# SBUF layout of a split-float matmul kernel: constants at the far end, packs and slots padded to 128 bytes

## The chip, the core and the metric

One core of a Trainium2 chip runs the whole program. The metric is the device time of one execution in microseconds (us), the median of the runs shown. TensorE (PE) multiplies, ScalarE (ACT) and VectorE (DVE) copy, split and combine, GpSimd (POOL) does small sums, SyncE (SP) issues every DMA. Each matmul has a stationary operand (128 columns, loaded first) and a moving operand (128, 256, 258 or 512 columns that stream past it), both read from SBUF.

## What is computed

A two-layer hybrid block (short convolution, gated MLP, sparse attention, convolution branch, then an FFN), followed by one block of another model (mLSTM with a Fourier branch, then a 16-expert MoE), on 256 tokens of width 1024, all in float32:

```python
def hybrid_layer(x, ...):                       # twice
    h = rmsnorm(x, g_mix)
    z = h @ w_in                                # 1024 x 2884
    ...                                         # four mixers y_a .. y_d
    x = x + concatenate([y_a, y_b, y_c, y_d], -1) @ w_out
    hf = rmsnorm(x, g_ffn)
    return x + (silu(hf @ w_gate) * (hf @ w_up)) @ w_down    # hidden 2816
# then rmsnorm, and second_block once:
    y, yc = token_mix(h, hc, lp, with_ctx)      # w_in 1024 x 1536, mLSTM, Fourier, w_out
    x = x + gate1 * rmsnorm_2(y, g_post_mix)
    for e in range(16):                         # hier_moe
        a = silu(h @ w_gate[e]) * (h @ w_up[e])
        y = y + combine[..., e, None] * (a @ w_down[e])
```

## The kernel before

**Split matmuls.** A large product is not done in the slow float32 mode. Each operand is split into a high part (rounded to float32r by ACT, L190) and a low part (the remainder, DVE, L191), and `mm3` (L234 to L241) adds three float32r products: high x high, high x low, low x high, pass by pass over the chunks of the contraction. The names end in `h`/`hi` and `l`/`lo`: `whi`, `wlo` are the weights, `xnh`, `xnl` a layer's input, `hfh`, `hfl` the FFN's input, `ffh`, `ffl` the FFN's hidden activations, `yah` to `ydl` the mixers' outputs, `hh`, `hl` the input of the second block, `m2h`, `m2l` its mixer output, `xgh`, `xgl` the tokens gathered for experts, `ahh`, `ahl` the experts' hidden activations, `oh` the one-hot columns that gather tokens from `h2h`, `h2l`. A plain float32 matmul stands on the timeline as two records.

**Which operand moves.** In `proj` (projections, FFN gate and up) and in the down and out products, the weights are stationary and 256 columns of activations move. In `proj_tok` (v and g_v) and in the whole MoE (L1308, L1335) it is the other way round: activations are stationary, and 256 or 512 columns of `whi`/`wlo` move.

**Stages.** Layer 0, FFN 0, layer 1, FFN 1 (with the ada modulation on DVE and the context's part woven in), the second block's mixer (`mixer2`), the MoE. An FFN has 11 groups: gate and up (96 matmuls of 256 columns), then down of the group before (48). An expert has 24 matmuls of 512 columns each for gate, up and down; the gates and ups are in two weight tiles each, the down too. Each weight tile is a DMA of 1 MB into a `raw` slot, a cast, a subtraction, and then its matmuls.

**Memory and order.** A tile framework places pools on a stack from the left end of SBUF (some, `side="right"`, from the right end) and writes all waits itself; the order on each engine comes from its scheduler with the priorities in the code (`later`). `const`, the first pool, holds small tiles (`ones`, `mhalf`, `inv256`, `warm`, `g0`, the pack `cst0`, `mod`): 3040 bytes of each partition, at the left end. `wraw`, `s8` (the 8 KB slots of the activations), `wsp` (`whi` and `wlo`, three buffers each) and the pools of the stages stack on it. `load_pack` (L174) loads a table of constants or parameters as one tile of as many columns as the table has. `rstd_row` keeps a 2-column tile `rsk` for a layer. The input of the second block has 258 columns a chunk (two more for a shift), so its slot in `s8` is 8256 bytes. `slot` (in `route`) is 8 floats a partition.

Of the kernel before, what the change touches and what calls it, by code (L numbers as in the profile page):

```python
# [11 lines left out]
F32 = mybir.dt.float32  # L12
# [5 lines left out]
P = 128  # L18
# [122 lines left out]
class Build:  # L141
    def __init__(self, ctx, tc, ins, out, offs, dbg=None):
        self.tc, self.nc, self.ins, self.out, self.dbg = tc, tc.nc, ins, out, dbg or {}
        self.offs, self.at = offs, {}
        pool = lambda name, bufs, **k: ctx.enter_context(tc.tile_pool(name=name, bufs=bufs, **k))
        self.const = pool("const", 1)
        self.wraw = pool("wraw", 3)
        self.psum = pool("psum", 1, space=bass.MemoryType.PSUM)
        self.pool = pool
        self.pending = None  # L150
        self.wx, self.wy, self.nraw = None, None, 0
# [20 lines left out]
        nc.scalar.activation(warm, self.ones[:, 0:1], AF.Square)  # L172

    def load_pack(self, name, pool, tag=None, bufs=1):  # L174
        t = pool.tile([P, self.ins[name].shape[1]], F32, tag=tag or name, name=name, bufs=bufs)
        self.nc.sync.dma_start(t, self.ins[name])
        for n, (o, m) in self.offs[name].items():
            self.at[n] = t[:, o:o + m]

    def p(self, name, i=None, n=1):  # L180
        return self.at[name] if i is None else self.at[name][:, i:i + n]
# [110 lines left out]
    def rstd_row(self, ps, n, eps, keep=None, direct=False):  # L292
        nc = self.nc
        if self.pending:
            self.pending()
            self.pending = None
        ms = self.tmp.tile([P, 2], F32, tag="ms", name="ms")
        nc.vector.tensor_scalar(ms, ps[:, 256:258], 1.0 / n, eps, op0=OP.mult, op1=OP.add)
        rs = (keep or self.tmp).tile([P, 2], F32, tag="rsk" if keep else "rs", name="rs", bufs=1 if keep else 2)
        nc.gpsimd.tensor_tensor(rs, ms, self.mhalf[:, 0, 0:2], op=OP.pow)  # L300
        for j in range(2):
            nc.tensor.matmul(ps[:, j * P:(j + 1) * P], rs[:, j:j + 1].to_broadcast([P, P]), self.c("ident"),
                             start=True, stop=True)
        if direct:
            return ps[:, 0:256]
        rb = keep.tile([P, 256], F32, tag="rbk", name="rbk", bufs=1) if keep else \
            self.tmp.tile([P, 256], F32, tag="t1", name="rb", bufs=self.t1)
        nc.scalar.copy(rb, ps[:, 0:256])
        return (rb, rs) if keep else rb
# [15 lines left out]
    def layer(self, l, x, X, sq):  # L325
# [274 lines left out]
        sqm = self.bank()  # L600
        H = self.bighl("hf")
        order = ((0, Ya), (2, Yc), (1, Yb), (3, Yd))
        for n, (j, Y) in enumerate(order):
            W = self.weights(w_out[:, j], 2, 1024, -4)
            for m in SPREAD:
# [4 lines left out]
                if n == 3:  # L610
                    tt(xm[:, m, :], acc[m // 2][:, m % 2, :], x[:, m, :], op=OP.add)
                    self.scaled_split(xm, p(f"g_ffn{l}", m), H, m)
                    self.sum_sq(sqm, xm[:, m, :], m, m == 7, 2)
        self.dump(f"xm{l}", xm)
        return xm, H, sqm

    def ffn(self, l, xm, H, sqm):
        nc, p = self.nc, self.p
# [4 lines left out]
        def gate_up(g):  # L623
            w_g = self.ins["w_gate"][l].rearrange("(k p) c -> p k c", p=P)[:, :, g * 256:(g + 1) * 256]
            w_u = self.ins["w_up"][l].rearrange("(k p) c -> p k c", p=P)[:, :, g * 256:(g + 1) * 256]
            psg = self.proj(self.weights(w_g, 8, 256), H, spread=SPREAD if g == 0 else None)
            if not rbs:
# [5 lines left out]
            nc.vector.tensor_tensor(gt, gt, rbb, op=OP.mult)  # L633
            psu = self.proj(self.weights(w_u, 8, 256), H)
            nc.vector.tensor_tensor(gt, psu, gt, op=OP.mult)
# [257 lines left out]
    def mixer2(self, x, sq):  # L893
# [4 lines left out]
        rb = self.rstd_row(sq, 1024, 1e-6, direct=True)  # L898
        xr = self.big("xr")
        sq2 = self.bank()  # L900
        H = self.bighl("h", (8, 258))
        nc.scalar.copy(H[0][:, :, 256:258], mod[:, 0:8, 0:1].to_broadcast([P, 8, 2]))
        tt(H[1][:, :, 256:258], mod[:, 0:8, 0:1].to_broadcast([P, 8, 2]), H[0][:, :, 256:258].bitcast(F32), op=OP.subtract)
        W = [self.weights(self.w_in2[:, :, g * 256:(g + 1) * 256], 8, 256, -4) for g in range(2)]
# [303 lines left out]
    def route(self):  # L1208
        nc, tmp, keep = self.nc, self.tmp, self.act
        small = lambda name, *shape: tmp.tile([P, *shape], F32, tag=name, name=name, bufs=1)  # L1210
        tt = nc.vector.tensor_tensor
        lt = small("lt", 5, 2, 4)
        for j in range(2):
            nc.vector.scalar_tensor_tensor(lt[:, :, j, :], self.lg[:, j * 20:(j + 1) * 20].rearrange("p (b i) -> p b i", b=5),
                                           self.rs2[j], self.brow.rearrange("p (b i) -> p b i", b=5),
                                           op0=OP.mult, op1=OP.add)
        v = lt.rearrange("p b j i -> p (b j) i")
        rank = self.ranks(v[:, 0:2], 2, "g")
        asg = tmp.tile([P, 2, 4], FR, tag="asg", name="asg", bufs=1)
        nc.vector.tensor_scalar(asg, rank, 0.0, None, op0=OP.is_equal)  # L1220
        own = asg.bitcast(F32)
        ps = self.bank()
        nc.tensor.matmul(ps[:, 0:8], self.striu, asg.rearrange("p j g -> p (j g)"), start=True, stop=False,
                         skip_group_check=True)
        nc.tensor.matmul(ps[:, 4:8], self.onesr, asg[:, 0], start=False, stop=True, skip_group_check=True)
        self.slot = keep.tile([P, 2, 4], F32, tag="slot", name="slot")
        nc.vector.tensor_scalar(self.slot, own, -1000.0, 1000.0, op0=OP.mult, op1=OP.add)
        self.slotted = tt(self.slot, self.slot, ps[:, 0:8].rearrange("p (j g) -> p j g", j=2), op=OP.add)
        for j in range(2):
            nc.tensor.matmul(ps[:, 8:12], self.onesr, asg[:, j], start=j == 0, stop=j == 1, skip_group_check=True)  # L1230
        gm, pe, psel = small("gm", 2), small("pe", 2, 4), small("psel", 2)
        nc.vector.tensor_reduce(gm, v[:, 0:2, :], AX.X, OP.max)
        tt(pe, v[:, 0:2, :], gm[:, :, None].to_broadcast([P, 2, 4]), op=OP.subtract)
        nc.scalar.activation(pe, pe, AF.Exp)
        nc.vector.tensor_reduce(psel, pe, AX.X, OP.add)
        nc.vector.reciprocal(psel, psel)
        ve = v[:, 2:]
        rank = self.ranks(ve, 8, "e")
        top, second = small("top", 8, 4), small("second", 8, 4)
        c1, c2, w1, w2 = small("c1", 8, 4), small("c2", 8, 4), small("w1", 8), small("w2", 8)  # L1240
        nc.vector.tensor_scalar(top, rank, 0.0, None, op0=OP.is_equal)
        nc.vector.tensor_scalar(second, rank, 1.0, None, op0=OP.is_equal)
        for w, c, o in ((w1, c1, top), (w2, c2, second)):
            tt(c, ve, o, op=OP.mult)
            nc.vector.tensor_reduce(w, c, AX.X, OP.add)
        tt(w2, w2, w1, op=OP.subtract)
        nc.scalar.activation(w2, w2, AF.Exp)
        nc.vector.tensor_scalar(w1, w2, 1.0, None, op0=OP.add)
        nc.vector.reciprocal(w1, w1)
        tt(w1.rearrange("p (g j) -> p g j", j=2), w1.rearrange("p (g j) -> p g j", j=2),  # L1250
           psel[:, None, :].to_broadcast([P, 4, 2]), op=OP.mult)
        tt(w2, w2, w1, op=OP.mult)
        for w, c, o in ((w1, c1, top), (w2, c2, second)):
            tt(c, o, w[:, :, None].to_broadcast([P, 8, 4]), op=OP.mult)
        tt(c1, c1, c2, op=OP.add)
        comb = small("comb", 2, 4, 4)
        tt(comb, c1.rearrange("p (g j) i -> p j g i", j=2), own[:, :, :, None].to_broadcast([P, 2, 4, 4]), op=OP.mult)
        self.split(comb, *(self.idc[:, :, o:o + 16].rearrange("p j (g i) -> p j g i", g=4) for o in (P, P + 16)))
        self.over = keep.tile([P, 5], mybir.dt.int32, tag="over", name="over")
        mxc = small("mxc", 1)  # L1260
        nc.vector.tensor_reduce(mxc, ps[:, 8:12], AX.X, OP.max)
        nc.vector.tensor_scalar(self.over[:, 0:4], ps[:, 8:12], 128.0, None, op0=OP.is_gt)
        nc.vector.tensor_scalar(self.over[:, 4:5], mxc, 128.0, None, op0=OP.is_gt)
# [287 lines left out]
```

## Time and profile before

| | us |
|---|---|
| three runs | 1147.66, 1145.09, 1141.58 |
| median | 1145.09 |
| span of the profiled execution, first to last instruction (its only time on the page) | 1141.0 |
| PE busy in it | 1081.2 (95%) |
| DVE busy | 894.8 (78%) |
| ACT busy | 644.1 (56%) |
| DMA engines, share of the span | 63.7% |

The profiled execution is 0.4% below the median and inside the three runs' own spread. A matmul's duration on the page is from its start to the end of its result, and neighbours overlap; what a stream of matmuls costs is the distance from start to start, which is read from the timeline: the start of the row after, less the start of the row, divided by the count.

### The profile page before, as it was taken

What the parts mean: (1) busy time and instruction counts of PE and PEld (TensorE: products, weight loads), DVE (VectorE), ACT (ScalarE), POOL (GpSimd) and SP (SyncE); (2) the same over time, 40 slices, a digit from 0 to 9 for tenths busy, and PEclk for the clock granted to TensorE, in tenths of its full rate; (3) what the DMA queues carried; (4) which work ended last, traced back from release to release, by engine and by line L of the source; (5) the groups of instructions that cost most, each with busy time, mean ns of one, the idle gap of its engine ahead of it and who ended that gap; (6) DMA issues with size and microseconds to landing.
All of it is one profiled execution on the core that took longest, in us unless ns stands there. A gap on an engine that the chain in (4) does not pass through costs nothing.

```text
span 1141.0 us, 18470 instructions
## 1 busy us (share of the span) xinstructions
PE 1081.2 (95%) x7384; PEld 981.0 (86%) x7384; DVE 894.8 (78%) x1449; ACT 644.1 (56%) x937; POOL 131.7 (12%) x139
## 2 busy tenths in 40 slices
PE   7998999999999989999999989899899999999995
PEld 6897999999998979899999988877778888878783
DVE  6897677887777976866877778765599898998976
ACT  5635654343455364635563345743587778777763
POOL 3091010000020830410000022000100000000001
PEclk9998999999999999999999989899989999999998
DMA  8734448677755254656678860420679699999981
GB/s 268 244 111 153 144 149 274 239 252 250 258 179 164 85 174 151 201 202 212 232 239 280 290 208 22 145 74 1 240 281 362 236 322 341 344 344 372 315 308 41
DMA packets 142126, 248.34 MB, mean 218 GB/s; under 512 B 6608, under 2 KB 84816, under 8 KB 142032
## 3 DMA queue, kind: packets, MB, share of 16 engines
q1 hardware_dynamic: 142032, 247.08, 63.7%
q8 instruction: 60, 0.98, 0.3%
q14 instruction: 34, 0.28, 0.1%
HBM read 246.01 MB, written 1.05 MB: 217 GB/s over the span
## 4 chain that ended last, share of the span: by engine, by line
PE 46%; DVE 4%; ACT 2%; issue 1%; POOL 1%; POOLq 0%; ACTq 0%; DVEq 0%
PE mm L240 24%; PE acc L240 14%; DVE wlo L191 1%; PE acc L919 1%; PE mm L1351 1%; PE mm L1278 1%; PE mm L729 1%; PE mm L1325 1%; PE mm L801 0%; POOL ssq L278 0%; PE mm L1060 0%; PE mm L1061 0%; PE mm L781 0%; DVE Mt L753 0%; PE mm L784 0%
## 5 line engine op out<-in xcount | busy, mean ns | idle before, releaser
L190 ACT CAST whi<-raw 128x1024 fp32r<-128x1024 f32 (+2 forms) x375 | 406.6, 1126 | 271.5 <-PE mm L240 130.8
L191 DVE TENSOR_TENSOR wlo<-raw,whi 128x1024 fp32r<-128x1024 f32 (+2 forms) x375 | 483.5, 1323 | 79.9 <-ACT whi L190 79.4
L240 PE MATMUL mm<-hfh,whi 128*128 128x256 f32 x672 | 94.6, 282 | 0.0
L240 PE MATMUL mm<-hfh,wlo 128*128 128x256 f32 x672 | 93.8, 282 | 0.0
L240 PE MATMUL mm<-hfl,whi 128*128 128x256 f32 x672 | 91.5, 278 | 0.0
L278 POOL TENSOR_TENSOR ssq<-ssq,sqt 128x256 f32<-128x256 f32 x40 | 37.6, 942 | 433.0 <-ACT sqt L270 428.7
L240 PEld LDWEIGHTS mm<-hfh,whi 128*128 128x128 f32 x672 | 85.7, 188 | 0.4 <-ACT whi L190 0.4
L240 PEld LDWEIGHTS mm<-hfh,wlo 128*128 128x128 f32 x672 | 85.4, 188 | 0.0
L240 PEld LDWEIGHTS mm<-hfl,whi 128*128 128x128 f32 x672 | 84.5, 188 | 0.0
L240 PE MATMUL mm<-whi,xgh 128*128 128x512 f32 x256 | 71.7, 399 | 0.5 <-ACT xgh L190 0.4
L240 PE MATMUL mm<-wlo,xgh 128*128 128x512 f32 x256 | 70.3, 395 | 0.0
L240 PE MATMUL acc<-ffh,whi 128*128 128x256 f32 x352 | 70.2, 280 | 0.0
L240 PE MATMUL mm<-whi,xgl 128*128 128x512 f32 x256 | 70.1, 395 | 0.0
L240 PE MATMUL acc<-ffh,wlo 128*128 128x256 f32 x352 | 69.8, 280 | 0.0
L240 PE MATMUL acc<-ffl,whi 128*128 128x256 f32 x352 | 69.4, 279 | 0.0
L692 DVE CUSTOM_DVE_ANT_0 araw<-araw,arow 128x1024 f32<-128x1024 f32 x48 | 58.3, 1228 | 0.0
L240 PEld LDWEIGHTS mm<-wlo,xgh 128*128 128x128 f32 x256 | 47.9, 187 | 11.9 <-DVE wlo L191 0.3
L240 PEld LDWEIGHTS mm<-whi,xgl 128*128 128x128 f32 x256 | 48.0, 187 | 11.7
L240 PEld LDWEIGHTS mm<-whi,xgh 128*128 128x128 f32 x256 | 46.9, 188 | 11.8 <-ACT xgh L190 1.3
L240 PEld LDWEIGHTS acc<-ffh,whi 128*128 128x128 f32 x352 | 54.0, 190 | 0.2
L240 PEld LDWEIGHTS acc<-ffh,wlo 128*128 128x128 f32 x352 | 54.1, 191 | 0.0
L240 PEld LDWEIGHTS acc<-ffl,whi 128*128 128x128 f32 x352 | 53.7, 190 | 0.0
(490 smaller groups left out, 2043.9 us busy)
## 6 DMA issues: line engine op xcount, KB each, us to landing
raw<-in_w_gate_dram SPq DMA_DIRECT2D x54, 1024.0 KB, 6.6
raw<-in_w_up_dram SPq DMA_DIRECT2D x54, 1024.0 KB, 6.8
raw<-in_w_down_dram SPq DMA_DIRECT2D x54, 1024.0 KB, 6.5
raw<-in_w_in_dram SPq DMA_DIRECT2D x29, 1024.0 KB, 5.2
araw<-in_w_adaT_dram SPq DMA_DIRECT2D x48, 512.0 KB, 5.0
raw<-in_w_out_dram SPq DMA_DIRECT2D x12, 1024.0 KB, 4.9
x<-in_xT_dram SPq DMA_DIRECT2D x4, 256.0 KB, 3.8
raw<-in_w_in_dram SPq DMA_DIRECT2D x4, 256.0 KB, 4.2
```

Source lines behind the costliest of these rows:

```text
L190: nc.scalar.copy(hi, src)
L191: nc.vector.tensor_tensor(lo, src, hi.bitcast(F32), op=OP.subtract)
L240: self.nc.tensor.matmul(out, w, x, start=start and i == 0, stop=stop and i == n - 1, **kw)
L278: nc.gpsimd.tensor_tensor(self.ssq, self.ssq, sq, op=OP.add)
L692: nc.vector.tensor_tensor_reduce(out, raw, rows[n], 1.0, 0.0, OP.mult, OP.add, self.mod[:, t, n:n + 1])
L729: nc.tensor.matmul(ps[0:100, :], self.weff[:, (c + 4) % 8, :], src, start=c == 0, stop=c == 7)
L919: nc.tensor.matmul(psx[m][:, 0:258], a, b[:, k, :], start=k == 0 and i == 0, stop=k == 7 and i == 2)
L1278: nc.tensor.matmul(ps[:, k * 256:(k + 1) * 256], self.H2[s][:, j, f], oh[:, j].rearrange("p n s -> p (n s)"), start=i == 0, stop=i == 3)
L1325: nc.tensor.transpose(ps[:, m * P:(m + 1) * P], ga[:, m * P:(m + 1) * P], self.c("ident"))
L1351: nc.tensor.matmul(ps, oT[:, j, :], Y[:, s, hf, :], start=s == 0, stop=s == 1)
```

## The change

Constants go to the right end of SBUF; the tables, `rsk` and `slot` get a size that is a multiple of 128 bytes, and so do the slots of `s8`, by way of the 264-column tile:

```diff
-        self.const = pool("const", 1)
+        self.const = pool("const", 1, side="right")
...
-        t = pool.tile([P, self.ins[name].shape[1]], F32, tag=tag or name, name=name, bufs=bufs)
-        self.nc.sync.dma_start(t, self.ins[name])
+        n = self.ins[name].shape[1]
+        t = pool.tile([P, -(-n // 32) * 32], F32, tag=tag or name, name=name, bufs=bufs)
+        self.nc.sync.dma_start(t[:, 0:n], self.ins[name])
...
-        rs = (keep or self.tmp).tile([P, 2], F32, tag="rsk" if keep else "rs", name="rs", bufs=1 if keep else 2)
+        rs = (keep or self.tmp).tile([P, 32 if keep else 2], F32, tag="rsk" if keep else "rs", name="rs",
+                                     bufs=1 if keep else 2)[:, 0:2]
...
-        H = self.bighl("h", (8, 258))
+        H = [t[:, :, 0:258] for t in self.bighl("h", (8, 264))]
...
-        self.slot = keep.tile([P, 2, 4], F32, tag="slot", name="slot")
+        self.slot = keep.tile([P, 2, 4, 4], F32, tag="slot", name="slot")[:, :, :, 0]
```

The instructions and their order are the same on all five engines, row by row. Four waits differ: the load of the pack `par2` loses one on DVE, the cast of `striu` (L1365) loses its waits, the matmul L1223 that uses it gains one on PE, and one 1 MB load of an early `w_up` tile of the MoE gains waits on PE and ACT.

What differs everywhere is where operands start. The built programs place them as follows (bytes, start address modulo 128; every chunk of a tile is a multiple of 128 bytes long unless noted):

| operand | part | before | after |
|---|---|---|---|
| `hfh`, `xnl` | moving, 256 columns | 96 | 0 |
| `hfl`, `xnh` | moving, 256 columns | 32 | 0 |
| `ffh`, `ffl`, `yah` to `ydl` | moving, 256 columns | 32 | 0 |
| `whi`, `wlo` | stationary (layers, FFN) and moving (MoE, `proj_tok`) | 96 | 0 |
| `hh`, `hl` (258 columns, k-th chunk) | moving | 32 + 8k, 96 + 8k | 32k |
| `xnh`, `xnl` in `proj_tok` | stationary | 32, 96 | 0 |
| `xgh`, `xgl` | stationary | 32 | 32 |
| `ahh`, `ahl` | stationary | 96 | 96 |
| `yo`, `oh` | moving | 96, 32 | 96, 32 |

## Rows read from the trace of the kernel before

**Rows 1.** Page, part 1: engine, busy us (share), instructions.

```profile
PE 1081.2 (95%) x7384; PEld 981.0 (86%) x7384; DVE 894.8 (78%) x1449; ACT 644.1 (56%) x937; POOL 131.7 (12%) x139
```

**Rows 2.** Page, part 4: the chain that ended last, by engine.

```profile
PE 46%; DVE 4%; ACT 2%; issue 1%; POOL 1%; POOLq 0%; ACTq 0%; DVEq 0%
```

**Rows 3.** Windows: stretch, length, busy PE, PEld, DVE, ACT, POOL; clock, DMA share, GB/s.

```profile
60.00:115.00 55.00, 49.77 (x397) 44.73 (x396) 44.61 (x98) 26.71 (x51) 26.61 (x29) 0.94 0.43 143
...
618.65:635.43 16.78, 16.78 (x147) 16.78 (x146) 13.11 (x16) 6.89 (x6) 0.00 (x0) 1.00 0.83 281
...
830.00:833.00 3.00, 3.00 (x14) 2.88 (x15) 3.00 (x14) 2.22 (x6) 0.00 (x0) 0.50 1.05 403
...
860.00:928.00 68.00, 68.00 (x305) 54.83 (x305) 62.83 (x65) 52.98 (x61) 0.00 (x0) 1.00 0.86 304
...
996.00:1064.00 68.00, 68.00 (x302) 54.75 (x301) 60.73 (x63) 49.13 (x56) 0.00 (x0) 1.00 0.99 354
```

**Rows 4.** Chain in order of time (start, us, what): FFN 1, mixer, an expert.

```profile
618.65 11.31 PE mm L240 x96
629.96 5.47 PE acc L240 x48
...
705.64 1.67 PE acc L919 x14
...
854.18 5.59 PE mm L240 x24
859.76 5.58 PE acc L240 x24
```

**Rows 5.** PE's timeline in FFN 1: start, us, line, tiles, count.

```profile
598.09 0.39 PE L240 MATMUL acc<-ffh,wlo 128*128 128x256 f32 x2
...
600.81 0.39 PE L240 MATMUL acc<-ffh,wlo 128*128 128x256 f32 x2
...
605.51 1.08 PE L240 MATMUL mm<-hfl,whi 128*128 128x256 f32 x8
606.43 1.12 PE L240 MATMUL mm<-hfh,wlo 128*128 128x256 f32 x8
607.38 1.11 PE L240 MATMUL mm<-hfh,whi 128*128 128x256 f32 x8
```

**Rows 6.** PE's timeline in layer 0: a projection, then plain float32 matmuls.

```profile
60.60 1.07 PE L240 MATMUL mm<-xnh,whi 128*128 128x256 f32 x8
61.51 1.12 PE L240 MATMUL mm<-xnl,whi 128*128 128x256 f32 x8
62.46 1.10 PE L240 MATMUL mm<-xnh,wlo 128*128 128x256 f32 x8
63.40 1.02 PE L375 MATMUL mm<-ropea,cst 128*128 128x512 f32 x2
64.26 1.02 PE L376 MATMUL mm<-ropeb,cst 128*128 128x512 f32 x2
```

**Rows 7.** PE's timeline in w_out: layer 1, first and last of its stretch.

```profile
440.60 0.40 PE L240 MATMUL acc<-ych,whi 128*128 128x256 f32 x2
...
441.78 0.40 PE L240 MATMUL acc<-ych,wlo 128*128 128x256 f32 x2
```

**Rows 8.** The same in layer 0.

```profile
129.04 0.39 PE L240 MATMUL acc<-ych,whi 128*128 128x256 f32 x2
...
131.76 0.39 PE L240 MATMUL acc<-ybh,whi 128*128 128x256 f32 x2
```

**Rows 9.** PE's timeline at the start of the MoE.

```profile
832.33 0.63 PE L1278 MATMUL mm<-oh,h2h 128*128 128x256 f32 x2
832.75 0.84 PE L1278 MATMUL mm<-oh,h2l 128*128 128x256 f32 x3
833.39 0.50 PE L1278 MATMUL mm<-oh,h2h 128*128 128x256 f32 x2
```

**Rows 10.** Who waited for whom on the DMA queue, 780 to 1141 us.

```profile
SPq L227 <- DVE wlo L191: 252.3, 87, 14.5
```

## Prediction

> **What bounds the kernel now.** First the busy shares: PE is busy 1081.2 of 1141.0 us, DVE 894.8, ACT 644.1 [rows 1]. Then the chain that ended last: 46% of the span is PE, 4% DVE, 2% ACT [rows 2]; the parts add up to a little over half, so it is followed back to about the middle of the program, and from there, in the second FFN and in the experts, it is matmul after matmul [rows 4]. The stretches say the same by stage: one FFN group of 16.78 us has PE busy for all 16.78, DVE for 13.11; 68 us of the MoE, four experts, have PE busy for all 68, DVE for 60.73 to 62.83, DMA engines for 0.86 to 0.99 of the time. Only the layers leave PE idle, 49.77 of 55 us [rows 3]. So in FFN and MoE a nanosecond less between two matmuls is a nanosecond less of span, until DVE or DMA is late.
>
> Next, what a matmul costs there. Column counts alone would give the same pace everywhere for 256 columns; the timeline doesn't. In the FFN's down product 24 matmuls (12 rows of two) take 2.72 us from 598.09 to 600.81, 113.3 ns each. In gate and up, eight with `hfh` moving take 0.95 us, 118.75 each, and eight with `hfl` 0.92, 115 each [rows 5]. In a layer `xnh` starts at 113.75, `xnl` runs at 118.75, and the pass after it, `xnh` again, at 117.5 [rows 6]. Held against the placements: a moving operand that starts at 32 of 128 bytes reaches 113.3, one at 96 never does, and after such a pass the one at 32 is slow for a while. At 2.4 GHz 256 columns are 106.7 ns, so 6.6 or 12 ns are lost each time. They are not lost at the low clock: in the stretch with a granted clock of 0.50, which is 1.2 GHz, five 256-column matmuls take 1.06 us, 212 each, and 256 columns at 1.2 GHz are 213 [rows 3, 9]. Nor in plain float32, which takes two cycles a column: 0.86 us for two records of 512 columns are 430 each, 0.42 ns a cycle [rows 6]. What is lost has to do with how fast operands are read at full speed, and there the start address may matter. That is the change's case, and it rests on two offsets, neither of which is 0.
>
> **The change, part by part.** No instruction is added, removed or moved, so every term is a change of pace.
>
> *What one matmul costs at offset 0* the trace does not show. The bounds: not below 107.5 ns for 256 columns and 215 for 512 (float32's 0.42 ns a cycle); above, 118.75 for 256, the pace of `hfh`. I take 113.3, the best that a steady run of split matmuls shows, and the nearest in kind. No 512-column split matmul moves from offset 32; the experts' move from 96 and take 5.59/24 = 232.9 ns in gate and up and 5.58/24 = 232.5 in down [rows 4]. I take two 256-column prices, 226.7.
>
> *FFN.* A group is 11.31 us for 96 gate and up matmuls (117.8 each) and 5.47 for 48 down (114.0 each) [rows 4]. At 113.3 it saves 96 x 4.5 ns + 48 x 0.7 ns = 0.46 us. Two layers of 11 groups: 22 x 0.46 = 10.1 us, all on the path. DVE's 13.11 us a group stay under the 16.3 that are left.
>
> *Layers.* Half a projection is 24 matmuls in 2.80 us [rows 6], 2.72 at 113.3, so a projection saves 0.16 us, the ten in a layer 1.6. `v` and `g_v` move weights, at 96: 96 x 5.4 ns = 0.5 us. w_out has 192 matmuls a layer, at 32 both times; in layer 1 ten take 1.18 us (118 each) and could save 0.9, in layer 0 24 take 2.72 and save nothing [rows 7, 8]. Sum for both layers 3.2 + 1.0 + 0.9 = 5.1 us. PE is idle for a tenth there and waits elsewhere for DVE's chain, so I count 0.7 of it: 3.6.
>
> *Second mixer and context.* 288 matmuls of 258 columns at 119.3 (14 in 1.67 us [rows 4]) against 114.2: 1.5 us, half of it on the path, 0.7. The context's projection, 96 x 5.4 ns = 0.5. w_out_2, 96 of 512 columns at 6 ns, 0.6. Together 1.8.
>
> *MoE.* 768 gate and up matmuls x 6.2 ns and 384 down x 5.8 ns: 4.8 + 2.2 = 7.0 us. What is late next: DVE at 15.2 to 15.7 us an expert (60.73/4, 62.83/4) against PE's 17.0, which would become 16.5; DMA delivers 354 GB/s there with its engines 0.99 busy [rows 3], while 6.29 MB in 16.5 us are 381. But the queue's issues wait for a slot to come free (252 us in all [rows 10]), so transfers follow PE's pace, and I let this gain stand whole.
>
> *The rest at nothing.* The four changed waits: the early `w_up` load that now waits for PE and ACT is queued before loads of the experts; behind it on SP stand only loads whose issues wait for slots anyway [rows 10], so a few us there are hidden, bound 0 to 3 us. ACT and DVE read and write the same tiles at the new offsets too; their durations I leave, since nothing shows an offset in them.
>
> Sum: 10.1 + 3.6 + 1.8 + 7.0 = 22.5 us of 1141.0, that is 1118.5; taken from the median, 4.1 us above that execution, 1145.1 - 22.5 = 1122.6. I say 1122.
>
> **The rivals.** *Full pace.* If a start at 0 takes the whole loss away, 107.5 and 215 ns: FFN 22 x (16.78 - 144 x 0.1075) = 28.6; layers 0.7 x (20 projections x 0.44 + 192 token matmuls x 11.2 ns + w_out 1.1 and 2.0) = 9.8; mixer, context and w_out_2 1.6 + 1.1 + 1.7; the MoE would save 18 ns x 1152 = 20.7 but DVE's 15.7 an expert and the DMA stop it near 16.0 of 17.0, so 16. Sum 59, time 1086. For it: the loss is in reading operands, and both offsets of before are 32 off a multiple of 64. Against it: no row of split matmuls below 113.3. The Trainium skill (TensorE: Matmul & The Clock Gate, Back-to-back issue gap) gives N/2.4 + 2.5 ns, by which 256 columns take 109.2 and 512 take 215.8 and the sum is, as an estimate, 51 us and the time 1094; no split matmul here runs so.
>
> *No change: the pace is a state, not an offset.* w_out in layer 1 runs at 118 for its whole stretch with operands that start at the same 32 and 96 as in layer 0, where it runs at 113.3 [rows 7, 8]. So an offset doesn't settle the pace; moving and stationary reads may fall into one rhythm or another by what ran before. If the new layout gets both, gains and losses cancel: 1145. The skill speaks for this one: by SBUF — State Buffer, Specifications (TRN2), a line of SBUF is 16 bytes, and 32, 96 and 0 are all multiples of 16, so the start of a 256-column operand would cost the same; the rows above, 113.3 against 118.75, don't agree with that as the whole story.
>
> *Slower: equal offsets collide.* Before, the fast case has moving at 32 and stationary at 96, half of 128 apart; `hfh` and `xnl` have both at 96 and run at 118.75. After, in every projection and FFN product both start at 0. If what costs is that both start at the same offset, all of FFN goes to 118.75: 144 x 118.75 = 17.10 us a group, 0.32 more, 22 x 0.32 = +7.0; the layers add 0.7 x (20 projections x 0.10 + w_out 1.05 and 0.14) = +2.2; experts' down, with both at 96, and gate and up, with 96 and 32, run alike today, so +0 there. Time 1154. It decides from 116.5 ns on, the mean of an FFN group today (16.78/144). Against it: the pass of `xnh` over `wlo` at 117.5 and w_out of layer 1 at 118 are slow with unequal offsets [rows 6, 7], so equality is at most one cause.
>
> **How the numbers follow.** Forecast 0.40, full pace 0.18, no change 0.18, equal offsets 0.24. 0.5% of the time, 5.7 us, is about what a measurement here can tell from nothing, so faster 0.58, same 0.18, slower 0.24. From 1090 to 1156 the range leaves out about half of the full pace's cases and a third of the slower ones, 0.17. The forecast alone would be 1112 to 1132.
>
> **What would show it.** Right: the FFN's chain pieces shrink from 11.31 to about 10.9 us for 96 and stay at 5.44 for 48; eight matmuls with `hfh` take 0.91 us on the timeline; 24 of an expert take 5.44. Full pace: 10.4, 5.2 and 5.2, and DVE's weight subtraction or DMA begins to end PE's waits in the MoE. No change: a mixture of 113 and 118 that doesn't follow the operands' names. Equal offsets: 48 down matmuls take 5.7 us. I'd be wrong altogether if the 512-column pace moves the other way from the 256-column one, or if ACT's casts or DVE's subtractions change their durations.

## The result and the profile after

The changed kernel takes a median of 1149.46 us (20 runs, 1145.72 to 1155.25), the kernel before on the same chip 1144.18 us (20 runs). The ratio is 1.0054, 95% interval 1.0038 to 1.0070: slower by some 5 us, where 22 us less were forecast. The profiled execution of the changed kernel took 1153.82 us with a span of 1152.0, 11.0 us longer than the span before.

The page of the changed kernel, busy times and the chain by engine (the counterparts of [rows 1] and [rows 2]):

```profile
PE 1096.2 (95%) x7384; PEld 995.6 (86%) x7384; DVE 895.6 (78%) x1449; ACT 643.4 (56%) x937; POOL 131.5 (11%) x139
...
PE 71%; DVE 11%; issue 6%; POOL 6%; ACT 4%; DMA 1%; SPq 0%; POOLq 0%; DVEq 0%; ACTq 0%
```

DVE, ACT and POOL have the same work as before to within 1 us. PE is busy 15.0 us longer with the same 7384 instructions, so each takes longer. (The chain's shares can't be compared: this one is followed back to the start of the program, the one before only to its middle.)

The chain of the changed kernel in order of time (start, us, what), where [rows 4] have 11.31 and 5.47 in FFN 1, and 5.59 and 5.58 in an expert (L241 is L240 of before):

```profile
627.96 11.52 PE mm L241 x96
639.48 5.76 PE acc L241 x48
...
864.89 5.60 PE mm L241 x24
870.49 5.60 PE acc L241 x24
```

Both FFN pieces are at exactly 120.0 ns a matmul (11.52/96, 5.76/48). A group takes 17.28 instead of 16.78 us, and 22 times 0.50 are 11.0 us. The experts' matmuls of 512 columns have the pace of before, 233 ns.

Where that lands by stage: windows of both kernels, cut where the first matmul of FFN 0, layer 1, FFN 1, the second mixer and the experts begins (columns as in [rows 3]). Before:

```profile
0.00:141.26 141.26, 124.86 (x913) 113.51 (x913) 105.86 (x218) 75.91 (x138) 43.13 (x53) 0.95 0.56 183
141.26:332.50 191.24, 188.92 (x1620) 188.51 (x1618) 151.13 (x176) 83.42 (x81) 7.99 (x8) 1.00 0.72 238
332.50:456.15 123.65, 117.86 (x913) 108.28 (x912) 98.25 (x207) 63.83 (x117) 42.22 (x41) 0.99 0.43 137
456.15:686.61 230.46, 220.55 (x1807) 217.36 (x1805) 169.99 (x233) 117.45 (x148) 22.53 (x19) 0.97 0.68 231
686.61:835.49 148.88, 137.06 (x838) 119.00 (x837) 103.75 (x335) 81.05 (x187) 11.47 (x15) 0.93 0.31 110
835.49:1141.00 305.51, 291.91 (x1306) 234.29 (x1304) 265.81 (x286) 222.46 (x270) 4.32 (x4) 0.98 0.85 296
```

After:

```profile
0.00:142.89 142.89, 127.49 (x913) 115.94 (x914) 105.70 (x218) 75.73 (x138) 42.99 (x53) 0.95 0.55 181
142.89:339.31 196.42, 194.36 (x1619) 193.95 (x1618) 151.30 (x176) 83.23 (x81) 8.01 (x8) 1.00 0.70 232
339.31:463.46 124.15, 119.53 (x914) 110.10 (x912) 98.41 (x207) 63.76 (x117) 42.30 (x41) 0.99 0.42 137
463.46:697.15 233.69, 225.32 (x1806) 222.19 (x1805) 170.64 (x233) 117.24 (x148) 22.36 (x19) 0.97 0.67 227
697.15:846.32 149.17, 137.35 (x838) 119.38 (x837) 103.89 (x335) 81.13 (x187) 11.49 (x15) 0.93 0.31 110
846.32:1152.00 305.68, 292.21 (x1306) 234.05 (x1304) 265.66 (x286) 222.33 (x270) 4.33 (x4) 0.98 0.84 296
```

Layer 0 loses 1.6 us, FFN 0 5.2, layer 1 0.5, FFN 1 3.2, the mixer 0.3, the experts 0.2. In FFN 1 PE is busy 4.8 us longer but waits 1.5 us less, which leaves 3.2.

**Why 11 in the profile and 5 in the medians.** These two executions had the same mean clock, 0.973. Over all executions a straight line through time and granted clock falls by 8.1 us per 0.01 of clock for the changed kernel (20 runs) and 8.4 for the kernel before (67 runs, those beside the experiments up to e9_all64_moe), and at 0.973 the lines stand at 1153.9 and 1143.9 us, 10.0 apart. But the median clock of the changed kernel is 0.978, that of those 67 runs of the kernel before 0.973. Those 0.005 are worth 4 us on the lines. So at one clock the changed kernel is some 10 us slower, and the medians are closer, the executions of the changed kernel having been granted a higher clock. That the slower pace is what raises the clock is a guess: no execution at 0.981 was profiled.

### The profile page after: what moved, and what is told of

It reads as the page before. It is cut to its first block, busy times and chain, and to the rows that moved or that the text cites. A ratio compares the mean times of both kernels' runs of the same rounds, so it can differ in the third digit from the quotient of the medians.

```text
span 1152.0 us, 18470 instructions
## 1 busy us (share of the span) xinstructions
PE 1096.2 (95%) x7384; PEld 995.6 (86%) x7384; DVE 895.6 (78%) x1449; ACT 643.4 (56%) x937; POOL 131.5 (11%) x139
## 4 chain that ended last, share of the span: by engine, by line
PE 71%; DVE 11%; issue 6%; POOL 6%; ACT 4%; DMA 1%; SPq 0%; POOLq 0%; DVEq 0%; ACTq 0%
PE mm L241 37%; PE acc L241 23%; DVE wlo L192 3%; POOL ssq L279 2%; POOL cv L428 1%; POOL ctap L427 1%; ACT whi L191 1%; DVE cv L430 1%; PE acc L417 1%; POOL rs L302 1%; PE acc L921 1%; PE mm L1353 1%; PE mm L1280 1%; PE mm L731 1%; PE mm L304 1%
## 5 line engine op out<-in xcount | busy, mean ns | idle before, releaser
L241 PE MATMUL mm<-hfh,whi 128*128 128x256 f32 x672 | 95.5, 284 | 0.0
L241 PE MATMUL mm<-hfl,whi 128*128 128x256 f32 x672 | 94.6, 283 | 0.0
L241 PE MATMUL mm<-hfh,wlo 128*128 128x256 f32 x672 | 94.3, 283 | 0.0
L241 PEld LDWEIGHTS mm<-hfh,whi 128*128 128x128 f32 x672 | 86.9, 192 | 0.4 <-ACT whi L191 0.4
L241 PEld LDWEIGHTS mm<-hfl,whi 128*128 128x128 f32 x672 | 86.7, 192 | 0.0
L241 PEld LDWEIGHTS mm<-hfh,wlo 128*128 128x128 f32 x672 | 86.7, 192 | 0.0
L241 PE MATMUL acc<-ffh,whi 128*128 128x256 f32 x352 | 72.2, 286 | 0.0
L241 PE MATMUL mm<-whi,xgh 128*128 128x512 f32 x256 | 71.7, 399 | 0.4 <-ACT xgh L191 0.3
L241 PE MATMUL acc<-ffh,wlo 128*128 128x256 f32 x352 | 71.8, 285 | 0.0
L241 PE MATMUL acc<-ffl,whi 128*128 128x256 f32 x352 | 71.5, 285 | 0.0
L241 PE MATMUL mm<-wlo,xgh 128*128 128x512 f32 x256 | 70.4, 396 | 0.0
L241 PE MATMUL mm<-whi,xgl 128*128 128x512 f32 x256 | 70.0, 395 | 0.0
L241 PEld LDWEIGHTS mm<-wlo,xgh 128*128 128x128 f32 x256 | 48.0, 188 | 11.8 <-DVE wlo L192 0.3
L241 PEld LDWEIGHTS mm<-whi,xgl 128*128 128x128 f32 x256 | 48.1, 188 | 11.7
L241 PEld LDWEIGHTS mm<-whi,xgh 128*128 128x128 f32 x256 | 46.9, 188 | 11.9 <-ACT xgh L191 1.3
L241 PEld LDWEIGHTS acc<-ffh,whi 128*128 128x128 f32 x352 | 55.5, 194 | 0.2
L241 PEld LDWEIGHTS acc<-ffh,wlo 128*128 128x128 f32 x352 | 55.6, 194 | 0.0
L241 PEld LDWEIGHTS acc<-ffl,whi 128*128 128x128 f32 x352 | 55.4, 194 | 0.0
```

Of the source, the lines that this page charges most:

```text
L241: self.nc.tensor.matmul(out, w, x, start=start and i == 0, stop=stop and i == n - 1, **kw)
```

## Experiments

The distance of two operands is here the moving operand's start address less the stationary one's. Theory going in: this distance, modulo 128 bytes, sets the pace; the change made it 0 in the projections and the FFN. Rivals: the absolute offset of one of them; no offset at all but a state of the queue; another part of the change.

**m1_map: the pace by offsets, by itself.** Its core (x and w are split once, `mo` and `so` are start offsets in bytes):

```diff
+    x = [t[:, mo // 4:mo // 4 + 2048].rearrange("p (k t) -> p k t", k=kc) for t in X]
+    w = [t[:, so // 4:so // 4 + 2048].rearrange("p (k t) -> p k t", k=8) for t in W]
...
+            for a, b in ((0, 0), (0, 1), (1, 0)):
+                for k in range(kc):
+                    nc.tensor.matmul(o, w[a][:, k, m * P:(m + 1) * P], x[b][:, k, 0:n], ...)
```

> A program of its own that leaves the whole reference out (it writes zeros and one unread product): after one split of a 1024 x 256 input and of a 1024 x 256 weight it runs steady streams of 256-column split matmuls in the three-pass order of L241, 96 at a time, for all 16 pairs of start offsets 0, 32, 64, 96 (mod 128 bytes) of moving and stationary operand, twice in opposite orders, then finer offsets, 512 columns and 128 columns. RELATION theory (only the distance of the two start offsets counts): pairs at equal offsets 120.0 ns a matmul (11.52 us per 96), pairs 64 apart 113.3 (10.88 us per 96), pairs 32 or 96 apart between or at 117.7; the absolute offsets make no difference. ABSOLUTE-MOVING rival: moving at 0 gives 120 and at 32 gives 113.3 whatever the stationary offset. ABSOLUTE-STATIONARY rival: the stationary offset decides alone. STATE rival (offsets don't matter, a queue settles in one of several paces): one pace for all 16 pairs, or paces that follow the order of the streams and differ between the two orders. 512 columns: 232 to 234 ns at all offsets by the rows of before and after.

Its chain in order of time; m is the moving, s the stationary start offset (a, c: 256 columns; d: 512):

```profile
59.36 11.52 PE am0s0z L50 x96
...
82.23 11.31 PE am0s64z L50 x96
...
138.98 11.31 PE am32s96z L50 x96
...
172.79 11.51 PE am64s64z L50 x96
...
452.02 5.44 PE cm112s0z L50 x48
...
463.15 5.45 PE cm192s0z L50 x48
...
497.25 5.68 PE cm16s16z L50 x48
...
530.82 5.45 PE dm32s32z L50 x24
...
541.86 5.60 PE dm32s96z L50 x24
547.46 5.51 PE dm64s0z L50 x24
```

Equal offsets run at 120 at 0, 32, 64 and 96 alike, so neither absolute offset alone decides. One equal pair does not: (16, 16) ran at 118.3, right after a stream at 113.3, and why is open. And 64 apart gives 117.8, not 113.3, with the very pair (32, 96) that the FFN of the kernel before ran at 113.3. 113.3 appears at (112, 0) and (192, 0). And one pair, (32, 0), ran at 117.8, 120.0 and 116.7 in three places; (96, 0), not equal, gave 120. So distance is right about most of the equal pairs, wrong as the whole story. A surprise: 512 columns run fastest at equal offsets, 227.0 against 233 at most others; 64 ahead, at (64, 0), comes near with 229.6.

**e1_w64: weights 64 bytes away.**

```diff
+        ph.enter_context(self.tc.tile_pool(name="gapa", bufs=1)).tile([P, 16], F32, name="gapa")
         self.wsp = ph.enter_context(self.tc.tile_pool(name="wsp", bufs=3))
+        ph.enter_context(self.tc.tile_pool(name="gapb", bufs=1)).tile([P, 16], F32, name="gapb")
...
-        H = [t[:, :, 0:258] for t in self.bighl("h", (8, 264))]
+        H = [t[:, :, 0:258] for t in self.bighl("h", (8, 260))]
```

> The changed kernel with only the weight tiles (whi, wlo) moved by 64 bytes: moving operands stay at 0, stationary at 64 (mod 128); everything behind them is put back by another 64 bytes, and to make room the rows of h are 260 columns long instead of 264. RELATION theory: all the 256-column split matmuls at 113.3 instead of 120.0 ns: an FFN group 16.32 instead of 17.28 us, 22 of them -21 us, layers and mixer some -5 us: 1120 to 1128 us, ratio to the kernel before 0.980 to 0.986. ABSOLUTE-MOVING rival (moving at 0 is the slow one): as the changed kernel, 1149 us, ratio 1.005, pieces of 96 at 11.52 us. STATE rival: somewhere at 117.9, about 1143 us, ratio 1.00.

Measured 1147.11 us, ratio 1.0038 (1.0014 to 1.0062). PE's timeline in FFN 1: first down row of a group, first gate row of the next, next down row:

```profile
599.23 0.40 PE L241 MATMUL acc<-ffh,whi 128*128 128x256 f32 x2
...
604.88 1.08 PE L241 MATMUL mm<-hfh,whi 128*128 128x256 f32 x8
...
616.16 0.40 PE L241 MATMUL acc<-ffh,whi 128*128 128x256 f32 x2
```

48 down matmuls in 5.65 us, 96 gate and up in 11.28: 117.7 and 117.5 ns, better than 120, far from 113.3. My expectation of 113.3 fell; the rival of a state had named 117.9.

**e2_const: only the constants moved.**

```diff
-        self.const = pool("const", 1)
+        self.const = pool("const", 1, side="right")
```

> The kernel before with only the constants moved to the right end: every start offset goes up by 32 mod 128 (weights 96 to 0, hfh and xnl 96 to 0, ff, xnh and hfl 32 to 64), the distances stay. RELATION theory: nothing changes, 1144 us, ratio 1.000 (0.997 to 1.003), pieces of 96 at 11.31 and of 48 at 5.47 us. ABSOLUTE-MOVING rival (0 slow, 32 fast): the pieces of 48 down (moving now at 64, not seen before) anywhere from 5.4 to 5.76 us, those of 96 (two of three passes at 0, the third at 64) at 11.5 us: 1149 us or more.

Measured 1143.77 us, ratio 0.9995 (0.9979 to 1.0011), with every absolute offset of the split matmuls changed and every distance kept. The same three places:

```profile
596.00 0.40 PE L240 MATMUL acc<-ffh,whi 128*128 128x256 f32 x2
...
601.47 1.12 PE L240 MATMUL mm<-hfh,whi 128*128 128x256 f32 x8
...
612.78 0.40 PE L240 MATMUL acc<-ffh,whi 128*128 128x256 f32 x2
```

5.47 and 11.31, the pieces of before. The moving operands `hfh` lie at a multiple of 128 here, and nothing is gained or lost by it.

**e3_eq64: all at 64, equal.**

```diff
+        ph.enter_context(self.tc.tile_pool(name="gapa", bufs=1)).tile([P, 16], F32, name="gapa")
         self.s8 = ph.enter_context(self.tc.tile_pool(name="s8", bufs=4))
...
-        H = [t[:, :, 0:258] for t in self.bighl("h", (8, 264))]
+        H = [t[:, :, 0:258] for t in self.bighl("h", (8, 260))]
```

> The changed kernel with everything from the slots of x on shifted by 64 bytes (rows of h 260 columns long, to make room): moving and stationary operands at 64, so none lies at a multiple of 128, all still at equal offsets. RELATION theory: as the changed kernel, 120.0 ns, pieces of 96 at 11.52 us, about 1149 us, ratio 1.005. ABSOLUTE-MOVING or ABSOLUTE-STATIONARY rival (the multiple of 128 itself is the slow place): 113 to 118 ns, 1120 to 1143 us.

Measured 1152.83 us, ratio 1.0069 (1.0046 to 1.0092); four runs; pieces of 11.47 and 5.76. The down matmuls, all at equal offsets away from 0, cost what they cost at 0. In gate and up only `hfh` is equal to the weights: modulo 256 `hfl` lies 128 away here, and these 96 matmuls take 11.47 instead of 11.52.

**m2_states: what ran ahead.** Streams as in m1_map, each behind a short stream:

```diff
+    for mo in range(0, 256, 16):
+        stream("preEz", 0, 0, 256, 1)
+        stream(f"Em{mo}s0z", mo, 0, 256, 2)
+    for mo in range(0, 256, 16):
+        stream("preFz", 64, 0, 256, 1)
+        stream(f"Fm{mo}s0z", mo, 0, 256, 2)
...
+        stream("Hz", 96, 96, 256, 4, lo=32)
+        stream("Iz", 32, 96, 256, 2)
...
+        stream("Jz", 32, 96, 256, 4)
+        stream("Kz", 32, 96, 256, 2)
```

> A program of its own that leaves the whole reference out, as m1_map. The map showed 120.0 ns at equal offsets, but at others 113.3, 116.7, 117.8, 118.3 or 120.0, and for one pair different paces at different times. Here each moving offset in steps of 16 bytes from 0 to 240 (stationary at 0) follows three predecessors: E, 24 matmuls at equal offsets; F, 24 matmuls 64 bytes apart; G, a wait for VectorE. Then the FFN patterns: H and I have the offsets of the kernel before (hi 96, lo 32, stationary 96; then 48 at 32), J and K have all moving operands 64 from the weights. SEVERAL-PACES theory (offsets allow some paces, the stream ahead picks one): 64 apart gives 113.3 behind E and 117.8 behind F or G; I gives 113.3, K 117.8; J 117.8. RELATION-AND-MOD-256 rival: the pace follows the offset modulo 256 alone, the same behind E, F and G (64 gives 117.8 and 192 gives 113.3). 512 columns: 227 to 229 at equal offsets, 233 at others.

Its chain in order of time:

```profile
97.51 5.66 PE Em64s0z L50 x48
...
123.31 5.50 PE Em112s0z L50 x48
...
165.93 5.46 PE Em192s0z L50 x48
...
230.77 2.72 PE preFz L50 x24
233.49 5.44 PE Fm64s0z L50 x48
...
301.04 5.65 PE Fm192s0z L50 x48
...
645.33 11.29 PE Hz L50 x96
656.62 5.46 PE Iz L50 x48
662.08 10.88 PE Jz L50 x96
672.96 5.44 PE Kz L50 x48
```

After a stream at equal offsets (E) a distance of 192 reaches 113.3 within its first matmuls, one of 64 stays at 117.8: what counts is the distance modulo 256, not 128. After a stream at 64 (F) 192 stays at 117.8, and 64 itself ran at 113.3 where the stream ahead of it already did (the rows of `preFz` and `Fm64`). So a distance allows certain paces, and the stream ahead picks one of them. Only 112 came to 113.3 after everything tried; 0, 80 and 96 gave 120. I has the down product's distance of the kernel before, 192, and J and K, with all moving operands at 192, run at 113.3 throughout, where 117.8 was expected. H was meant to have the kernel's gate and up, and has them only modulo 128: modulo 256 its high part is at distance 0, the kernel's `hfh` at 128. That its piece, 11.29 us, is within 0.02 of the kernel's is a coincidence of sums: on the timeline its three passes take 0.96, 0.93 and 0.94 us, those of the kernel 0.95, 0.92 and 0.95. Both theories named ahead were half right. Series G tells nothing more than E, since PE filled its wait with five matmuls of another stream. Here 64 was as good as equal offsets for 512 columns (5.50 us for 24 at (64, 0) and at (0, 0), 5.60 at (32, 0)), so equality is not their only fast distance.

**e4_moe0, e5_x64, e6_ff64** had their expectations written before m2_states was known. e4_moe0 pads two small tiles so that `xg` and `ah` start at 0 mod 128:

```diff
-        self.over = keep.tile([P, 5], mybir.dt.int32, tag="over", name="over")
+        self.over = keep.tile([P, 32], mybir.dt.int32, tag="over", name="over")[:, 0:5]
...
-        cw = self.act.tile([P, 4], F32, tag="cw", name="cw", bufs=2)
+        cw = self.act.tile([P, 16], F32, tag="cw", name="cw", bufs=2)[:, 0:4]
```

> The changed kernel with the experts' stationary tiles (xg, ah, and oT) moved so that they also start at 0 mod 128, by padding two small tiles ahead of them. By the map (227 to 229 ns for 512 columns at equal offsets, 233 at others) a piece of 24 falls from 5.60 to about 5.47 us: 96 of them -12 us, less where an expert waits for its weights: 1138 to 1146 us, ratio 0.995 to 1.003. RIVAL (the map's 512-column streams don't carry over, since the weights alternate and the experts wait for transfers): pieces of 24 stay at 5.60, 1149 us, ratio 1.005.

Measured 1148.83 us, ratio 1.0022 (1.0000 to 1.0044), which is 0.3% below the changed kernel's 1.0054, though the two intervals overlap. The window of its experts' stage is clearer, 301.60 us where the changed kernel has 305.68:

```profile
849.20:1150.80 301.60, 288.06 (x1306) 234.60 (x1304) 265.38 (x286) 222.57 (x270) 4.33 (x4) 0.98 0.85 300
```

Modulo 256 only `xg` lies at the weights' offset, `ah` is 128 away, and only `xg` gained: its matmuls start 227 to 229 ns apart, those of `ah` 232 to 233.

e5_x64 has gapa ahead of the slots and gapb ahead of wsp, e6_ff64 has gapb alone behind wsp, both with h at 260 columns:

```diff
+        ph.enter_context(self.tc.tile_pool(name="gapa", bufs=1)).tile([P, 16], F32, name="gapa")
         self.s8 = ph.enter_context(self.tc.tile_pool(name="s8", bufs=4))
...
+        ph.enter_context(self.tc.tile_pool(name="gapb", bufs=1)).tile([P, 16], F32, name="gapb")
         self.wsp = ph.enter_context(self.tc.tile_pool(name="wsp", bufs=3))
```

> The changed kernel with the slots of x, xn, hf moved by 64 bytes alone (weights, ff and y stay at 0; rows of h 260 columns long): gate and up projections run 64 apart, down at equal offsets. SEVERAL-PACES theory: the down projection at 120.0 leaves the queue in the state from which 64 apart runs at 113.3: pieces of 96 at about 10.9 us, of 48 at 5.76, an FFN group 16.6 us against 16.78 before and 17.28 after: about 1135 to 1141 us, ratio 0.993 to 0.998. RIVAL (64 apart is 117.8 here as in e1_w64): pieces of 96 at 11.3, group 17.07, 1145 us, ratio 1.002.

> The changed kernel with ff and y (and all behind them) moved by 64 bytes alone; x, xn, hf and the weights stay at 0; rows of h 260 columns long: gate and up at equal offsets, down 64 apart. SEVERAL-PACES theory: gate and up at 120.0 (11.52 us per 96), and behind them down at 113.3 (5.44 us per 48): group 16.96, about 1142 to 1146 us, ratio 0.999 to 1.003. RIVAL (down at 117.8): 5.65 us per 48, group 17.17, 1147 us.

Measured 1147.83 us, ratio 1.0032 (1.0016 to 1.0049), and 1147.45, ratio 1.0039 (1.0018 to 1.0060). PE's timeline of e6_ff64:

```profile
600.27 0.40 PE L241 MATMUL acc<-ffh,whi 128*128 128x256 f32 x2
...
605.92 1.13 PE L241 MATMUL mm<-hfh,whi 128*128 128x256 f32 x8
...
617.39 0.40 PE L241 MATMUL acc<-ffh,whi 128*128 128x256 f32 x2
```

Down at 5.65 us instead of the 5.44 expected; in e5_x64 gate and up took 11.29 instead of 10.9. Both theories missed and their rivals, 117.8, came out, because the theories took distances modulo 128. Modulo 256 `ff` lies at a distance of 64 from the weights in e6_ff64 and e1_w64, which in m2_states left 117.8 only where the stream ahead ran at 113.3. And slots of 260-column rows are 8320 bytes, 32.5 times 256, so `hfh` and `hfl` lie 128 apart: in e5_x64 and e1_w64 `hfh` is at 192 and starts at 114 to 116, then `hfl`, at 64, brings 117.8, and nothing leaves it again.

**e7_undo, e8_all64, e9_all64_moe: the distances alone.** In the changed kernel, xn and hf are put at chosen bytes of their 8448-byte slots, and the packs unpadded, which puts `ff` and the mixers' outputs `ya` to `yd` at a distance of 192 from the weights:

```diff
+        at = {"xn": (192, 128), "hf": (128, 192)}.get(name)
+        if at:
+            return tuple(self.big(name + s, (2048 + 48,), FR)[:, o // 4:o // 4 + 2048].rearrange("p (a b) -> p a b", a=8)
+                         for s, o in zip("hl", at))
...
-        t = pool.tile([P, -(-n // 32) * 32], F32, tag=tag or name, name=name, bufs=bufs)
+        t = pool.tile([P, n], F32, tag=tag or name, name=name, bufs=bufs)
```

e8_all64 has 192 four times; e9_all64_moe also has the padding of `over` and `cw` ([P, 32] here), by which `xg` and `ah` both lie at the weights' offset mod 256.

> The changed kernel (constants at the right end, padded slots, rows of h 264 columns long) with only the distances between moving and stationary operands put back to those of the kernel before, taken mod 256: xn and hf are placed 128 or 192 bytes into their slots and the packs are not padded, so that ff and y lie 192 behind the weights again. SEVERAL-PACES theory, distances taken mod 256: as the kernel before, pieces of 96 at 11.31 and of 48 at 5.47 us, 1144 us, ratio 0.998 to 1.002. RIVAL (another part of the change, its waits, the right end or the slots, costs the 5 us): 1149 us, ratio 1.004 to 1.006, or the pieces as before and the time lost elsewhere.

> As e7_undo, but xn and hf, hi and lo, all start 192 bytes into their slots, so that every moving operand of the projections lies 64 bytes short of the weights mod 256 (the distance of J and K in m2_states, which ran at 113.3 throughout). SEVERAL-PACES theory: if the queue enters the fast pace, 113.3 for all: pieces of 96 at 10.9, of 48 at 5.44 us, an FFN group 16.32 against 16.78 us before, -10 us, and some -3 in the layers: about 1131 us, ratio 0.987 to 0.992. If nothing ahead kicks it over (no stream at equal offsets is left in the FFN), it stays at 117.8 with the other stable pace: 16.97 a group, 1147 us, ratio 1.002 to 1.004. RELATION rival (distance 64 gives 117.8 in the whole kernel as in e1_w64): the latter.

> As e8_all64, with the experts' stationary tiles xg and ah moved to the same start offset mod 256 as the weights that stream past them (in e4_moe0 xg was equal mod 256 and ran at 227 to 229 ns, ah equal only mod 128 and ran at 232 to 233). Theory: xg and ah both at 227 to 229 against 233 ns: up to 2304 x 5 ns = 11.5 us below e8_all64, less where an expert waits for its weights; 3 to 8 us expected (e4_moe0 gave some 4 for xg alone). RIVAL: ah stays at 232 to 233, as e4_moe0: 3 to 4 us below e8_all64.

e7_undo: 1145.18 us, ratio 1.0009 (0.9986 to 1.0031). Its three places in FFN 1 give pieces of 5.48 and 11.30:

```profile
599.87 0.40 PE L245 MATMUL acc<-ffh,whi 128*128 128x256 f32 x2
...
605.35 1.12 PE L245 MATMUL mm<-hfh,whi 128*128 128x256 f32 x8
...
616.65 0.40 PE L245 MATMUL acc<-ffh,whi 128*128 128x256 f32 x2
```

With the old distances in layers and FFN the loss is gone, while the constants, the slots, the rows of `h` and the experts' operands stay as the change has them. What the rest of the change costs is not distinguishable from 0.

e8_all64: 1138.17 us, ratio 0.9959 (0.9931 to 0.9988), between the two values named ahead, 1131 and 1147. Its profiled execution, the fastest of its twelve, has 10.88 and 5.44 us in the FFN's late groups, span 1131.5. But its runs spread from 1133 to 1147, and at one clock, 0.970, from 1136 to 1147. That would fit a layout where what ran ahead picks the pace; it is not shown, since only one execution was profiled.

e9_all64_moe: 1129.3 us, ratio 0.9891 (0.9852 to 0.9930), 8.9 us below e8_all64 where 3 to 8 were expected. Its chain, and the window of its experts' stage:

```profile
612.29 10.88 PE mm L245 x96
623.17 5.44 PE acc L245 x48
...
843.93 5.47 PE mm L245 x24
849.40 5.44 PE acc L245 x24
...
826.04:1124.70 298.66, 285.36 (x1306) 234.13 (x1304) 264.72 (x286) 222.35 (x269) 4.33 (x4) 0.98 0.85 303
```

The experts run at 227 to 228 ns, `ah` included, and their stage takes 298.66 us instead of 305.51 before. This version beats both kernels, by 1.1% and 1.6%.

**e10_112**: as e9_all64_moe with 112 for xn and hf.

```diff
-        at = {"xn": (192, 192), "hf": (192, 192)}.get(name)
+        at = {"xn": (112, 112), "hf": (112, 112)}.get(name)
```

> As e9_all64_moe, but xn and hf start 112 bytes into their slots instead of 192: the one distance (112 mod 256) that ran at 113.3 in m2_states behind all three predecessors. SEVERAL-PACES theory: the layers' projections, which in e9_all64_moe ran at 114 to 118, come to 113.3 to 114 (some 820 matmuls by 2 to 3 ns, -2 us), gate and up in both FFNs at 113.3; the down projections (192 behind the weights) enter either stable pace: at 113.3, about 1127 us, ratio 0.986 to 0.989; at 117.8, 22 pieces of 48 by 0.21 us more, about 1132 us, ratio 0.989 to 0.992. RIVAL (112 is fast only for the streams of the map): pieces of 96 at 11.2 us or more, 1135 us or more.

Measured 1132.6 us, ratio 0.9900 (0.9878 to 0.9923): pieces of 10.96 and 5.44, which in the forecast went with 1127 us, not with 1132. In a projection of layer 1, 40 matmuls take 4.53 us, 113.3 ns each. Where the other 5 us lie was not followed; the profiled execution had a granted clock of 0.968, that of e9_all64_moe 0.976. It is as good as e9_all64_moe within the intervals, and its six runs spread by 6.5 us (1129.8 to 1136.3) against 11.4.

## Why the prediction was wrong

**The price at offset 0** is the step that failed. It took 113.3 ns, "the best that a steady run of split matmuls shows, and the nearest in kind"; measured are 120.0, above even the bound of 118.75 that was set from the pace of `hfh`. The rows held the better answer: `hfh` and `xnl` over the weights were the 256-column cases with equal offsets modulo 128, and they were the slow ones. The prediction saw that, wrote it down as the rival "equal offsets collide", and set it aside because unequal offsets were slow too ([rows 6, 7], 117.5 and 118). By m2_states they had another reason: their distance of 192 has a second stable pace, 117.8. That equality is not the only cause was no evidence that it is harmless. And `hfh` was 128 away modulo 256, where the pace alternates (118.5 to 118.8 in m2_states), so that rival's price too was 1.25 ns low.

**Term by term.** *FFN*: forecast -10.1, measured +8.4 us (5.2 + 3.2). *Layers*: -3.6, measured +2.1, near the rival's +2.2. *Mixer and context*: -1.8; the mixer's stage lost 0.3. *MoE*: -7.0, measured +0.2. The step that failed there is the same, two 256-column prices for 512 columns: `xg` and `ah` stayed away from the weights' offset (32 and 96 modulo 128 against 0), and 233 ns stayed. The 7 us were there to be had, and e9_all64_moe took 6.9 of them, by equal offsets. That its 226.7 ns (5.44/24) are just twice 113.3 is luck: the equal offsets that give it cost 120.0 with 256 columns. *The rest at nothing* held: the four waits and the padding cost nothing that e7_undo or the stages show, and DVE's and ACT's durations stayed.

**The rivals.** "Slower: equal offsets collide", at 1154 with a chance of 0.24, is what happened, in its mechanism and its place; the sum of +9.2 us stands against +11.0 of span, and the median is lower, at a higher granted clock, for which no term stood. That 1149 lies inside the range of 1090 to 1156 is owed to the part kept for this rival, not to the forecast. "No change: a state, not an offset" named the second half of the truth, that one distance runs at several paces; m2_states shows both at work. "Full pace" never showed: no stream of 256 columns, in any placement tried, held a pace below 113.3. The Trainium skill gives N/2.4 + 2.5 ns (TensorE: Matmul & The Clock Gate, Back-to-back issue gap) for an isolated matmul; the prediction took it for a stream. As an estimate from it 256 columns take 109.2 ns and 512 take 215.8, and no stream here reached either, with 113.3 and 226.7 at best. By the Trainium skill a line of SBUF is 16 bytes (SBUF — State Buffer, Specifications (TRN2)). The prediction drew from it that all these offsets would cost the same, and they don't: 113.3 to 120.0 between offsets that are all multiples of 16.

**What bounds the kernel** was read rightly: an FFN group is its 144 matmuls back to back at 16.32 us (e9_all64_moe), 16.78 and 17.28, and in the experts PE did not wait longer at the faster pace (stage less PE busy: 13.6 us before, 13.3 in e9_all64_moe).

## What to carry to other kernels

Before aligning tiles to a round number, look at which operands of one matmul end up at the *same* offset, and take distances modulo 256 bytes: with 256 columns streaming the same offset was among the slowest (120.0 ns, but for one pair), with 512 columns the fastest in the kernel (227 against 233). When the trace shows a slow and a fast case and a change makes everything like neither, price the new case by the row that shares its *relation*, not by the best row. A pace that depends on what ran ahead needs streams in the kernel's own order to be measured: in m1_map the pair (32, 96) gave 117.8 where the kernel had 113.3.

## What was not expected of the hardware

- Most steady streams settle at one of a few paces: 113.3, 116.7, 117.8, 118.3 and 120.0 ns for 256 columns, and 123 at an offset of 4 bytes (5.91 us for 48 in m1_map). Two of them can be stable for one pair of offsets.
- 128 columns at four pairs of offsets take 110.6 to 111.7 ns, almost what 256 columns take at best, so half a moving operand saves nearly nothing. Why is not shown; the trace only shows that each matmul has a weight load beside it, of 192 ns at all four pairs. With 256 columns this load takes 192 ns at the equal offsets 0, 32, 64 and 96, and 187 to 189 in the other streams that start at multiples of 16.
- Which reads get in each other's way is open. The runs show that the distance of the two start addresses and what ran ahead matter, not by which rule, and the pair (16, 16) shows that these two may not be all.
